# Retention's gated output stored as halves and read in groups, more down-projection tiles kept on chip, and the work around both down projections reordered

## The chip, the cores and the metric

The kernel runs on one core of a Trainium2 chip. The metric is device time of one launch, in microseconds (us); lower is better. The median of three runs of the kernel before is 2861.47 us (2861.45 to 2865.29).

## The reference

One inference step of a two-layer streaming encoder over T = 1056 rows (1024 prompt rows of a new stream and 32 rows of a running one), all in float32, model width D = 1024:

```
layer 0:  x += Retention(RMSNorm(x));  x += ConvFFN(RMSNorm(x))
layer 1:  x += GLA(RMSNorm(x));        x += ConvFFN(RMSNorm(x));  then a final RMSNorm
retention: q, k, v, g = h @ w_in; per head S = gamma^L S + k^T v, o = intra + q S
           out = (silu(g) * groupnorm(o)) @ w_out          (w_out: 2048 x 1024, "w_ro")
gla:       the same form with gates per channel; out = (silu(r) * rmsnorm(o)) @ w_out   (1024 x 1024, "w_go")
conv_ffn:  u = h @ w_up; a causal convolution of width 3; silu(gate) * val @ w_down
```

The outputs are y, the new retention and GLA states and the new convolution caches.

## The kernel before, in words

TensorE multiplies float32 as sums of shorter products: each factor is split into a high half (a cast on ACT) and a low half (a subtraction on DVE), and each product is three matmuls (high x high, high x low, low x high; lines 1311 to 1313 in `Down.run`). A weight tile is 128 x 1024 ("K tile", 512 KB): `load_w` (L97 to 102) loads it into one of three `raw` tiles and splits it into `whi` and `wlo`, out of a ring of ten `w` tiles.

The stages, in us of the profiled execution: projections of the retention to 349; four retention heads of 87 us each to 697; the retention's down projection to about 900; FFN up and down of layer 0 to 1630; GLA to 2045; its down projection to about 2129; FFN of layer 1 to the end. The change touches the heads, both down projections and the two entries to an FFN.

**The heads** (`retention`, L440 and on). Each head goes through nine steps of 128 rows (eight of the prompt, one of the sample). A step computes scores, output and state update on TensorE; DVE and ACT normalise the output (`output`: bn_stats L585, square root L589, `on` L599); a step later `norm` transposes it (`pt`, L604), multiplies it by the gate (`ot`, L609) and stores it to HBM as float32 (`scr_or`, L610). `update` (L630) forms the new state `Sn`. The last head's last gated tile stands in a kept `w` tile named `or`. While the last steps run, `early` (L1250) already loads and splits K tiles 0 and 1 of the down projection, and `order` pins some of those instructions behind others on the same engine. PSUM banks have tags (`sm`, `v`, `out`, two buffers each, and a projection bank).

**The down projections** (class `Down`, L1242 to 1363). The rows go in four chunks of 264 (`CQ`). For each chunk `run` goes through the K tiles (16 of w_ro, 8 of w_go), each with eight output tiles, so 24 matmuls of 264 columns per K tile, and accumulates in eight PSUM banks. In layer 0, `load` fetches a K tile's 132 KB of gated output (`HR<-scr_or`, L1285), splits it (`XH`, L1286 and L1287) and loads and splits its weights. K tiles 5 to 7 of w_ro (0 to 2 of w_go) stay on chip in `XB` after their first use; all others are loaded again for each chunk. In layer 1 the gated output is stored as halves already (`scr_hg`), and a 1056 KB group of four K tiles comes by one load on POOL's queue (L1278). At a chunk's last K tile each output tile is evicted right behind its matmuls (`evict`: residual added on DVE, L1498; square sums on ACT; two tiles at a time stored to `scr_x` by POOL, L1502). The next chunk starts with its first tiles (`hold`: four) in seven banks; the eighth holds the row sum `pn` of the chunk before (L219), from which DVE (`rm`, L225) and ACT (L164, L165) form 1/rms, `R`. Then `done` scales the chunk by the norm's weights and R, eight DVE instructions of 128x264 (L1515), and `x_sums` (L288 to 293) forms and splits the sums and differences for the FFN. Such deferred pieces are emitted two or three per K tile (`later`).

**The entry to an FFN** (`ffn_up`, L1365). Its products use seven instead of eight block products (`seven`), with sums of weights (`weight_sums`: L312 to 323) and of x. `weight_sums(0)` is called when the down projection has been emitted; the last chunk's norm comes behind the fourth product.

A scheduler places the instructions of each engine by emission order and priority; `order` adds constraints. Each engine and each DMA queue (SP's, POOL's) then runs in order.

Of the kernel before, what the change touches and what calls it, by code (L numbers as in the profile page):

```python
# [50 lines left out]
def trunk_kernel(ctx: ExitStack, tc: tile.TileContext, io):  # L51
# [45 lines left out]
    def load_w(src, dst=None, after=None, queue=nc.sync):  # L97
        i = uid()
        raw = raw_tile(f"raw{i}")
        queue.dma_start(raw, src)  # L100
# [111 lines left out]
    def rms_row(ss, c0, n, ps, after=None, join=False):  # L212
# [12 lines left out]
        V.tensor_scalar(m_, ps, 1.0 / D, EPS, op0=ALU.mult, op1=ALU.add)  # L225
        rsqrt(r_, t_, m_)

# [152 lines left out]
    scr_o = [io["scr_or"], io["scr_og"]]  # L380
# [34 lines left out]
    def retention():  # L415
# [29 lines left out]

        def rsm(name):
            return pp.tile([P, 512], F32, tag="sm", name=name, bufs=2)
# [18 lines left out]
        for h in range(RH):  # L466
# [5 lines left out]
            def before(m):  # L472
# [15 lines left out]
                if samp and h + 1 == RH:  # L488
                    kept = w_tile("or").bitcast(F32)
                    sg = kept[:, RDV:RDV + 4 * L].rearrange("p (e t) -> p e t", e=4)  # L490
# [4 lines left out]
                pss = pp.tile([P, 512], F32, tag="sm", name=f"pss{i}", bufs=2)  # L495
# [13 lines left out]
                pk = pp.tile([P, 2, P], F32, tag="sm", name=f"pk{i}", bufs=2)  # L509
# [16 lines left out]
                psv = pp.tile([P, RDV], F32, tag="v", name=f"psv{i}", bufs=2)  # L526
# [29 lines left out]
            def output(ctx):  # L556
# [12 lines left out]
                po = pp.tile([P, RDV], F32, tag="out", name=f"po{i}", bufs=2)  # L569
# [7 lines left out]
                else:  # L577
# [7 lines left out]
                V.bn_stats(bs[:L], po[:L])  # L585
# [7 lines left out]
                V.scalar_tensor_tensor(ab[:L, 3:4], mv[:L, 0:1], -1.0, ab[:L, 2:3],  # L593
                                       op0=ALU.mult, op1=ALU.mult)
                if kept is not None:
                    on = kept[:, :RDV]
# [4 lines left out]
                def norm(sm, i=i, on=on, L=L, t0=t0, h=h, sg=sg, kept=kept):  # L601
# [3 lines left out]
                    if kept is not None:  # L605
                        ot = kept[:, RDV + 4 * L:RDV + 8 * L].rearrange("p (e t) -> p e t", e=4)
                    else:
                        ot = rp.tile([P, 4, P], F32, tag="ot", name=f"ot{i}", bufs=2)
                    V.tensor_tensor(ot[:, :, :L], pt[:, :, :L], sg, op=ALU.mult)  # L609
# [3 lines left out]
                return last_root, ts, last_on  # L613

            def update(ctx, after=None):
# [20 lines left out]
                if m >= 7:  # L636
                    dst = io["o_ret_p"] if m == 7 else io["o_ret_s"]
                    nc.sync.dma_start(dst[h].rearrange("(d p) e -> p d e", p=P), sn)
# [7 lines left out]
            root7, ts7, on7 = output(c7)  # L646
# [7 lines left out]
        norms[0](lambda name: pp.tile([P, 512], F32, tag="v", name=name, bufs=2))  # L654
# [253 lines left out]
    def gla(closers):  # L908
# [147 lines left out]
        def mix(h, c, u):  # L1056
# [109 lines left out]
            def store(lv, room):  # L1166
                for e in range(2):
# [5 lines left out]
                    nc.sync.dma_start(scr_o[1][2 * h + e, :, c0:c0 + n], ot[:, :n])  # L1173
# [68 lines left out]
    class Down:  # L1242
        def __init__(self, nk, wsrc, hsrc, chunks, res, sm, keep, hold):
# [3 lines left out]
            self.banks = self.after = self.groups = None  # L1247

        def early(self, kt, after=None, wafter=None):
# [4 lines left out]
            h = w_tile(f"hs{uid()}")  # L1254
            ins = (S.copy(h[:, :n], hr),
                   V.tensor_tensor(h[:, 512:512 + n], hr, h[:, :n].bitcast(F32), op=ALU.subtract))
            if after is not None:
                for a, b in zip(ins, after):
                    order(a, b)
# [504 lines left out]
```

## Time and profile before

| | us |
|---|---|
| median of 3 runs | 2861.47 |
| profiled execution | 2860.82 |
| its span, first to last instruction | 2859.0 |
| TensorE (PE) busy | 2818.5, 99% |
| VectorE (DVE) busy | 1976.2, 69% |
| ScalarE (ACT) busy | 1333.7, 47% |
| GpSimd (POOL) busy | 297.7, 10% |

The page gives one execution: busy time by engine, the granted clock of TensorE, DMA, groups of instructions by line. Views of the trace answer for a stretch: busy time, what an engine waited for, single instructions in time. Matmuls overlap in the pipeline, so a matmul's own duration (0.28 us for 264 columns) is longer than the pace at which they start.

### The profile page before, as it was taken

What the parts mean: (1) busy time and instruction counts of PE and PEld (TensorE: products, weight loads), DVE (VectorE), ACT (ScalarE), POOL (GpSimd) and SP (SyncE); (2) the same over time, 40 slices, a digit from 0 to 9 for tenths busy, and PEclk for the clock granted to TensorE, in tenths of its full rate; (3) what the DMA queues carried; (4) which work ended last, traced back from release to release, by engine and by line L of the source; (5) the groups of instructions that cost most, each with busy time, mean ns of one, the idle gap of its engine ahead of it and who ended that gap; (6) DMA issues with size and microseconds to landing.
All of it is one profiled execution on the core that took longest, in us unless ns stands there. A gap on an engine that the chain in (4) does not pass through costs nothing.

```text
span 2859.0 us, 51822 instructions
## 1 busy us (share of the span) xinstructions
PE 2818.5 (99%) x20670; PEld 2721.2 (95%) x20670; DVE 1976.2 (69%) x3313; ACT 1333.7 (47%) x2402; POOL 297.7 (10%) x558
## 2 busy tenths in 40 slices
PE   9999999999999999999999999999999999999998
PEld 8999988887999999999999999999989999999998
DVE  7876666666688878787555677775488777876544
ACT  7444444444554444444444555553344444444443
POOL 0000000000020111111000122220131111110000
PEclk9999999999999999999999999999999999999999
DMA  5333444333873222223755411115651222227544
GB/s 221 100 117 105 148 120 131 106 107 113 276 227 120 82 83 75 83 75 114 251 186 174 129 37 41 46 44 199 230 180 60 90 68 90 69 81 250 184 155 145
DMA packets 199890, 365.72 MB, mean 128 GB/s; under 512 B 34976, under 2 KB 133408, under 8 KB 198368
## 3 DMA queue, kind: packets, MB, share of 16 engines
q1 hardware_dynamic: 195232, 344.00, 37.2%
q0 software_dynamic: 3856, 17.83, 1.8%
q8 instruction: 161, 2.64, 0.4%
q14 instruction: 81, 0.66, 0.1%
q10 hardware_dynamic: 560, 0.59, 0.1%
HBM read 279.07 MB, written 83.28 MB: 127 GB/s over the span
## 4 chain that ended last, share of the span: by engine, by line
PE 89%; DVE 6%; DMA 2%; ACT 2%; issue 1%; SPq 0%; POOL 0%; DVEq 0%; ACTq 0%; POOLq 0%
PE pu L357 14%; PE pu L352 13%; PE pu L356 13%; PE pd L1311 8%; PE pd L1312 7%; PE pd L1313 7%; PE psv L245 2%; PE psv L246 2%; PE psv L247 2%; PE pj L770 1%; DMA raw<-w_ro 1%; PE pg L123 1%; PE pg L124 1%; PE pl L1024 1%; PE pg L125 1%; PE pj L123 1%
## 5 line engine op out<-in xcount | busy, mean ns | idle before, releaser
L102 DVE TENSOR_TENSOR wlo<-raw,whi 128x1024 fp32r<-128x1024 f32 x226 | 282.1, 1251 | 247.9 <-ACT whi L102 237.3
L102 ACT CAST whi<-raw 128x1024 fp32r<-128x1024 f32 x226 | 236.0, 1049 | 319.5 <-PE pd L1312 227.5
L1311 PE MATMUL pd<-hh,whi 128*128 128x384 f32 (+1 forms) x880 | 285.0, 324 | 0.0
L1312 PE MATMUL pd<-hl,whi 128*128 128x384 f32 (+1 forms) x880 | 284.3, 323 | 0.1
L1313 PE MATMUL pd<-hh,wlo 128*128 128x384 f32 (+1 forms) x880 | 283.9, 323 | 0.0
L333 ACT COPY HR<-pu 128x264 f32<-128x264 f32 x264 | 98.9, 375 | 313.1 <-PE pu L357 310.6
L357 PE MATMUL pu<-XA,wgl 128*128 128x264 f32 x752 | 213.4, 284 | 0.0
L352 PE MATMUL pu<-XA,wgh 128*128 128x264 f32 x752 | 212.6, 283 | 0.0
L356 PE MATMUL pu<-XA,wgh 128*128 128x264 f32 x752 | 212.4, 283 | 0.0
L1312 PEld LDWEIGHTS pd<-hl,whi 128*128 128x128 f32 x880 | 165.7, 188 | 0.9 <-DVE hl L1287 0.4
L1311 PEld LDWEIGHTS pd<-hh,whi 128*128 128x128 f32 x880 | 165.7, 188 | 0.4
L1394 DVE SCALAR_TENSOR_TENSOR AR<-AR,cw 128x1058 f32<-128x1058 f32 x88 | 115.9, 1317 | 72.3 <-ACT AR L1393 72.3
L1313 PEld LDWEIGHTS pd<-hh,wlo 128*128 128x128 f32 x880 | 165.6, 188 | 0.1
L1311 PE MATMUL pd<-XH,whi 128*128 128x264 f32 x560 | 160.2, 286 | 0.5 <-DMA XH<-scr_hg 0.5
L1313 PE MATMUL pd<-XH,wlo 128*128 128x264 f32 x560 | 158.9, 284 | 0.0
L1312 PE MATMUL pd<-XH,whi 128*128 128x264 f32 x560 | 158.8, 284 | 0.1
L313 DVE TENSOR_TENSOR wtl<-rv,wth 128x1024 fp32r<-128x1024 f32 x58 | 71.0, 1225 | 117.1 <-ACT wth L312 115.4
L1374 DVE TENSOR_TENSOR AR<-HR,pu 128x264 f32<-128x264 f32 (+2 forms) x440 | 144.5, 367 | 4.6 <-PE pu L357 4.6
L352 PEld LDWEIGHTS pu<-XA,wgh 128*128 128x128 f32 x752 | 141.2, 188 | 0.0
L356 PEld LDWEIGHTS pu<-XA,wgh 128*128 128x128 f32 x752 | 141.2, 188 | 0.0
L357 PEld LDWEIGHTS pu<-XA,wgl 128*128 128x128 f32 x752 | 141.0, 188 | 0.0
L352 PE MATMUL pu<-XA,wsh 128*128 128x264 f32 x464 | 132.3, 285 | 4.4 <-ACT wsh L312 3.2
(483 smaller groups left out, 9585.3 us busy)
## 6 DMA issues: line engine op xcount, KB each, us to landing
raw<-w_down SPq DMA_DIRECT2D x120, 512.0 KB, 3.6
raw<-w_ro SPq DMA_DIRECT2D x55, 512.0 KB, 4.5
rg<-w_up SPq DMA_DIRECT2D x44, 512.0 KB, 3.5
rv<-w_up SPq DMA_DIRECT2D x44, 512.0 KB, 3.5
scr_h<-AR SPq DMA_DIRECT2D x44, 512.0 KB, 2.6
HR<-scr_h SPq DMA_DIRECT2D x84, 192.0 KB, 3.6
raw<-w_go SPq DMA_DIRECT2D x23, 512.0 KB, 4.0
scr_x<-AR POOLq DMA_DIRECT2D x32, 264.0 KB, 4.0
```

The costliest lines, as they stand in the source:

```text
L102: ins = S.copy(hi, raw), V.tensor_tensor(lo, raw, hi.bitcast(F32), op=ALU.subtract)
L123: PE.matmul(ps, hi[:, k], rh, start=kt == 0, stop=False)
L313: V.tensor_tensor(l_, src, h.bitcast(F32), op=ALU.subtract)
L333: S.copy(t, b)
L352: mm = PE.matmul(ps, wh[:, k], x[:, 0, kt], start=m in (1, 2, 4, 5) and kt == 0, stop=False, skip_group_check=True)
L356: PE.matmul(ps, wh[:, k], x[:, 1, kt], start=False, stop=False, skip_group_check=True)
L357: mm = PE.matmul(ps, wl[:, k], x[:, 0, kt], start=False, stop=kt == 3, skip_group_check=True)
L1311: PE.matmul(o, w[0][:, k], h[0][:, :n], start=i == 0, stop=False)
L1312: PE.matmul(o, w[0][:, k], h[1][:, :n], start=False, stop=False)
L1313: self.last_mm = PE.matmul(o, w[1][:, k], h[0][:, :n], start=False, stop=i == nk - 1)
L1374: V.tensor_tensor(u[:, d:d + n], t[:, o:o + n], b[:, o:o + n], op=op)
L1394: V.scalar_tensor_tensor(cj, uj[:, 1:T + 3], cw[:, nt, 1:2], cj, op0=ALU.mult, op1=ALU.add)
```

## The change

1. `norm` in the heads gates in place, splits the result (an ACT cast and a DVE subtraction of 128x512 per step, 35 in all, into one buffer `hl`) and stores both halves to `scr_hr`, laid out by chunk and group (44 stores, since a step that crosses a chunk's border is stored in two). The down projection of layer 0 then reads groups of 1056 KB by POOL, as layer 1 does: 16 loads instead of 62 of 132 KB, and no splits. The state stores of the last head go by POOL's queue.
2. More weights stay on chip. In layer 0, K tiles 3 and 8 to 11 stay through chunk 1, 2 and 4 through chunk 2, 5 to 7 throughout, with a new order of K tiles in chunks 1 to 3: w_ro is loaded 46 times instead of 55. In layer 1 all eight tiles of w_go stay: 8 loads instead of 23. Every fourth load of layer 0's chunks 1 to 3 goes into `HR`, free now, as a fourth raw tile (7 loads).
3. Orders and banks at the last head's end: seven PSUM tags in fixed places (`bank`), state updates and weight splits behind the last two steps' `bias`, the gating of step 7 ahead of the last update; chunk 0 starts in two halves of four banks instead of three and five.
4. Orders in the chunks: the eight evictions come behind all eight matmul groups, the next chunk's first two low halves behind the last eviction and later ones behind `rm`, and the next chunk's groups are asked for ahead of time, the stores to `scr_x` behind them on POOL. Layer 1 holds three K tiles instead of four before `pn`.
5. `weight_sums(0)` of the FFN is emitted inside the last chunk, two K tiles before its last in layer 1, before the last in layer 0. In the order of DVE's instructions, layer 0's sums stood ahead of the last evictions before as well, layer 1's did not.
6. The norm's weights g are multiplied on by ACT (eight of 128x264 per chunk, in `pre`, ahead of the row sum), and R by DVE in two instructions of 128x1056.

TensorE's instructions are the same in number. The core of the diff:

```diff
-                    V.tensor_tensor(ot[:, :, :L], pt[:, :, :L], sg, op=ALU.mult)
-                    nc.sync.dma_start(scr_o[0][4 * h:4 * h + 4, :, t0:t0 + L].rearrange("e p t -> p e t"),
-                                      ot[:, :, :L])
+                    gated = V.tensor_tensor(ot[:, :, :L], pt[:, :, :L], sg, op=ALU.mult)
+                    if after is not None:
+                        order(gated, after)
+                    cast = S.copy(hl[:, :, 0, :L], ot[:, :, :L])
+                    V.tensor_tensor(hl[:, :, 1, :L], ot[:, :, :L], hl[:, :, 0, :L].bitcast(F32), op=ALU.subtract)
...
+                        nc.sync.dma_start(io["scr_hr"][c, h, :, :, :, o:o + n], hl[:, :, :, a:a + n].bitcast(F32))
...
-            sn7 = update(c7, ts7)
+            sn7 = update(c7, ts7 if h + 1 < RH else bias7)
...
-                d1s[0].early(1, (root7, ts7), (root7, sn7))
-                d1s[0].after = on7, sn7
-            output(c8)
-            update(c8)
+                d1s[0].early(1, (root7, sn7))
+            _, _, bias8 = output(c8)
+            if h + 1 == RH:
+                d1s[0].after = last_on, bias8
+                norms[0](lambda name: bank("v", name), bias8)
+            update(c8, bias8 if h + 1 == RH else None)
...
+        def group(self, c, q):
+            if (c, q) not in self.groups:
+                h = self.room("hq").rearrange("p (k j t) -> p k j t", k=4, j=2)
+                self.asked = G.dma_start(h, self.gsrc(c, q))
+                self.groups[c, q] = h
+            return self.groups[c, q]
...
+            w = self.kept.get(kt)
+            if w is None:
+                dst = self.room("kw") if kt in self.keep else None
+                if c == 0 and kt in self.homes:
+                    home = self.homes[kt][0]
+                    dst = home[:, :D], home[:, D:2 * D]
...
+                if self.put is not None:
+                    self.count += 1
+                    after = None, self.put if self.count < 3 else self.rm
+                    self.loads += 1
+                    if self.spare is not None and self.loads % 4 == 3:
+                        raw = self.spare[:, :D], self.steps[-5]
+                elif self.spare is not None and kt in range(4, 7):
+                    after = self.gated
+                w = load_w(self.wsrc(kt), dst, after, raw=raw)
+                if dst is not None or self.stay:
+                    self.kept[kt] = w
...
+                    if ask and i == nk - 3:
+                        self.group(c + 1, ask[0])
...
+                    if c == len(self.chunks) - 1 and i == nk - 1 and not self.stay:
+                        nxt_sums()
                     if prev is None or i > J:
                         for nt in range(KT):
                             mm(i, nt)
-                            if i == nk - 1:
-                                evict(c, nt, xr[:, nt], ps[nt][:, :n], ss)
+                        if c == len(self.chunks) - 1 and i == nk - 3 and self.stay:
+                            nxt_sums()
+                        if i == nk - 1:
+                            if ask:
+                                self.group(c + 1, ask[1])
+                            for nt in range(KT):
+                                self.put, self.count = evict(c, nt, xr[:, nt], ps[nt][:, :n], ss), 0
...
+                            if pre is not None:
+                                pre(last)
+                            dg[0] = self.rm = norm_a(c - 1, prev)
...
+            def pre(xr):
+                for kt in range(KT):
+                    S.activation(xr[:, kt], xr[:, kt], AF.Copy, scale=gcol[:, idx, kt:kt + 1])
...
-                        V.scalar_tensor_tensor(a, a, gcol[:, idx, kt:kt + 1], R[:, c0:c0 + n],
-                                               op0=ALU.mult, op1=ALU.mult)
...
+                        V.tensor_tensor(a, a, R[:, c0:c0 + n].unsqueeze(1).to_broadcast([P, 4, n]), op=ALU.mult)
...
+            go([lambda after: (pre(xr), norm(3, ss, after))] + done(3, xr), down.early, d1.last_mm)
...
+    d1s[0].kts = {c: [5, 6, 7, 4, 2, 3, 0, 1] + list(range(8, 16)) for c in range(1, 4)}
+    d1s[1].stay, d1s[1].kts = True, {3: [3, 0, 1, 4, 5, 6, 7, 2]}
+    d1s[0].banks = (0, 1, 2, 3), (4, 5, 6, 7)
```

More of the change, by code (lines that the diff above doesn't have):

```diff
@@ L95, in w_tile, with load_w @@
         return wp.tile([P, D], F32R, tag="w", name=name, bufs=10)
-    def load_w(src, dst=None, after=None, queue=nc.sync):
+    def load_w(src, dst=None, after=None, queue=nc.sync, raw=None):
         i = uid()
-        raw = raw_tile(f"raw{i}")
-        queue.dma_start(raw, src)
+        behind = None
+        if raw is None:
+            raw = raw_tile(f"raw{i}")
+        else:
+            raw, behind = raw
+        load = queue.dma_start(raw, src)
+        if behind is not None:
+            order(load, behind)
         hi, lo = dst or (w_tile(f"whi{i}"), w_tile(f"wlo{i}"))
@@ L1301, in run @@
                     kts = list(keep) + [k for k in kts if k not in keep]
+                kts = self.kts.get(c, kts)
+                for k, (_, end) in self.homes.items():
+                    if c > end:
+                        self.kept.pop(k, None)
                 J = self.hold
@@ L1533, in second_room @@
+            ss, todo, xr = d1.run(droom, evict, norm, None, done, (), sums, pre)
+            later(todo, len(todo))
+            go([lambda after: (pre(xr), norm(3, ss, after))] + done(3, xr), down.early, d1.last_mm)
         def second_room(dp):
```

193 lines of the change are left out of this document (104 added, 89 removed).

## The prediction

> **What bounds the kernel now.** I read the head of the page first, then a table of busy time by stretch around the two places that the change touches (the down projection of the retention, 697 to 930 us, and that of the GLA with the entry to its FFN, 1960 to 2165 us), and then TensorE's own list of waits in both.
>
> ```profile
> span 2859.0 us, 51822 instructions
> PE 2818.5 (99%) x20670; PEld 2721.2 (95%) x20670; DVE 1976.2 (69%) x3313; ACT 1333.7 (47%) x2402; POOL 297.7 (10%) x558
> ```
>
> TensorE is busy for 2818.5 of 2859.0 us. The change takes no matmul away, so only idle and slowly clocked stretches can be won. The columns of the next table are the stretch, its length, busy time and instructions of PE, PEld, DVE, ACT and POOL, the granted clock, the DMA share and GB/s.
>
> ```profile
> 610.00:697.00 87.00, 86.81 (x423) 70.54 (x422) 54.45 (x129) 33.63 (x67) 0.00 (x0) 1.00 0.28 79
> 697.00:721.00 24.00, 21.25 (x156) 18.70 (x155) 14.27 (x28) 12.52 (x19) 0.33 (x2) 1.00 0.80 268
> 721.00:749.00 28.00, 28.00 (x233) 28.00 (x232) 17.05 (x24) 14.77 (x24) 0.00 (x0) 1.00 0.93 300
> 749.00:757.00 8.00, 6.08 (x49) 5.68 (x48) 7.28 (x15) 5.85 (x13) 3.41 (x5) 1.00 0.81 254
> 757.00:800.00 43.00, 43.00 (x355) 42.94 (x354) 30.02 (x49) 20.55 (x33) 4.14 (x7) 1.00 0.79 270
> 800.00:850.00 50.00, 48.77 (x398) 48.28 (x397) 41.61 (x60) 28.77 (x48) 13.05 (x17) 1.00 0.63 202
> 900.00:926.00 26.00, 23.03 (x169) 22.04 (x169) 23.94 (x36) 9.75 (x16) 1.43 (x2) 0.95 0.12 38
> 2070.00:2113.00 43.00, 42.19 (x344) 41.59 (x343) 37.05 (x56) 20.93 (x33) 16.50 (x23) 1.00 0.71 236
> 2113.00:2119.00 6.00, 4.52 (x36) 4.25 (x35) 5.97 (x8) 2.76 (x5) 4.24 (x8) 1.00 0.35 105
> 2131.00:2142.00 11.00, 7.07 (x34) 6.53 (x34) 8.48 (x11) 4.93 (x9) 2.53 (x4) 0.69 0.47 156
> 2152.00:2165.00 13.00, 10.69 (x79) 9.63 (x78) 12.12 (x14) 6.92 (x9) 0.00 (x0) 1.00 0.12 42
> ```
>
> The stretch from 757 to 800 is the undisturbed pace: 43.00 us for 355 matmuls of 264 columns, 0.1211 us each, so 2.91 us for the 24 of a K tile. Against that pace each stretch loses its length less its matmuls times 0.1211: 2.1 us at 749 (8 - 49 x 0.1211), 1.8 at 800 to 850, 5.5 at 900 to 926, 1.3 at 2070 to 2113, 1.6 at 2113 to 2119, 6.9 at 2131 to 2142 and 3.4 at 2152 to 2165. At 697 to 721 other shapes are mixed in, and I take the idle time, 2.75. In sum 25.4 us can be won, 0.9% of the run. Part of it is no wait but clock: at 900 to 926 a granted 0.95 costs 26 x 0.05 = 1.3 us, at 2131 to 2142 a granted 0.69 costs 3.4.
>
> What TensorE waits for, first from 697 to 930, then from 2060 to 2165 (total, times, longest, in us):
>
> ```profile
> PE pd L1311 <- DVE AR L1498: 3.0, 3, 1.5
> PE pu L352 <- DVE AR L1374: 1.3, 2, 1.1
> PE pt L604 <- ACT or L599: 1.1, 1, 1.1
> PE pd L1311 <- DVE Sn L630: 1.0, 1, 1.0
> PE pu L352 <- ACT HR L333: 0.9, 1, 0.9
> PE pu L356 <- DVE XB L289: 0.7, 1, 0.7
> PE pt L604 <- ACT on L599: 0.6, 1, 0.6
> ```
> ```profile
> PE pu L352 <- ACT wsh L312: 3.2, 1, 3.2
> PE pd L1311 <- DVE rm L225: 1.5, 1, 1.5
> PE pu L352 <- ACT HR L333: 0.9, 1, 0.9
> PE pd L1311 <- DMA XH<-scr_hg: 0.5, 1, 0.5
> ```
>
> They are handovers between stages: the last head to the down projection (or, Sn, on), eviction of a chunk's last banks (L1498), the norm chain into the FFN (L1374, L289, L333), and in layer 1 the split of the FFN's weight sums (wsh). None is throughput of DVE or ACT.
>
> **The heads: 0 us.** Each 128-row step gains an ACT cast and a DVE subtraction of 128x512, priced by the same shapes:
>
> ```profile
> 562.38 0.69 DVE L609 TENSOR_TENSOR ot<-pt,sg 128x512 f32<-128x512 f32 x1 [2.67 <-PE pt L604]
> 562.00 0.59 ACT L540 CAST vh<-psv 128x512 fp32r<-128x512 f32 x1 [2.89 <-PE psv L247]
> ```
>
> So 0.59 us more on ACT and 0.69 on DVE per step, against idle stretches of 2.89 and 2.67 us just before these rows: the cover is about 2 us a step, and the head's 87 us keep 0.2 us of idle. If that cover were gone, 35 steps would cost up to 1.28 us each, 45 in all; I take 0, bounded by +2 for the few steps that carry weight splits too. The stores double to 512 KB:
>
> ```profile
> scr_or<-ot SPq DMA_DIRECT2D x32, 256.0 KB, 2.4
> raw<-w_ro SPq DMA_DIRECT2D x55, 512.0 KB, 4.5
> XH<-scr_hg POOLq DMA_DIRECT2D x6, 1056.0 KB, 6.0
> scr_x<-AR POOLq DMA_DIRECT2D x32, 264.0 KB, 4.0
> AR<-xT SPq DMA_DIRECT2D x4, 1056.0 KB, 9.2
> ```
>
> At 2.4 us for 256 KB an estimate for 512 KB is 4.8, and the single buffer is wanted again after 87/9 = 9.7 us, on queues that are 0.28 busy. The fixed PSUM banks leave TensorE's order in the heads as it was.
>
> **Entry to the down projection: -1.0 us (-2.7 to +1.3).** on (0.6) and Sn (1.0) should go: the last two steps' biases now stand ahead of the state updates on DVE, and K tile 0 gets four banks that aren't held by Sn. The wait for or (1.1) stays and may grow: its gating on DVE now comes behind a 0.69 subtraction, and ACT has 0.59 ahead of it. I count -1.6 + 0.6. The last state stores move from SP's to POOL's queue; the first write into the room that they free is the split of K tile 4, some ten us later, against a landing like the 4.0 of POOL's other stores.
>
> **Chunk feed: 0 us.** Per chunk the 16 loads of 132 KB and their splits become four POOL loads of 1056 KB that need no splits, and w_ro falls from 55 loads to 46, w_go from 23 to 8. In chunk 0 it is no relief: 24 us x 268 GB/s + 28 x 300 = 14.8 MB moved from 697 to 749; now 14 x 0.13 = 1.9 MB go and 2.1 to 4.2 come (two groups can be fetched before 697). At 300 GB/s that is 1 to 8 us more of transfers in a stretch that was 0.93 busy. With a K tile per 2.91 us a group feeds 11.6 us, and 6.0 to 9.2 us of landing fit, so I take 0, and keep the price of the miss for the rivals.
>
> **Chunk boundaries: -3.3 us in layer 0 (-3.9 to -1.5), -2.0 in layer 1 (-2.9 to -0.5).** The eight evictions now go to DVE back to back, and the next chunk's first splits are held behind the last of them, where before a split stood between. What is lost at 749 and 800 to 850 is 3.9 us; I leave 0.2 per boundary. In layer 1 (2.9 lost) w_go stays on chip, so no split is left there at all; but the norm's row sum is asked for after three K tiles (8.7 us) instead of four, which may be early for its last sum on POOL. I leave 0.3 per boundary. Next to that, ACT gets eight scalings per chunk; behind them stand weight splits that the order places K tiles ahead of need.
>
> **Exit of layer 0: -0.9 us (-2.5 to +2).** The scaling falls from 8 instructions to 2:
>
> ```profile
> L102 DVE TENSOR_TENSOR wlo<-raw,whi 128x1024 fp32r<-128x1024 f32 x51 | 64.1, 1259 | 18.5 <-ACT whi L102 18.4
> L1515 DVE SCALAR_TENSOR_TENSOR AR<-AR,gcol,R 128x264 f32<-128x264 f32 x32 | 13.7, 486 | 0.0
> L293 DVE TENSOR_TENSOR AR<-AR 128x1056 f32<-128x1056 f32 x8 | 10.0, 1249 | 0.0
> ```
>
> 8/32 of 13.7 is 3.4 us; two of 128x1056 take 2.5. The 0.9 gained comes off the waits for XB (0.7) and HR (0.9). For it, ACT does eight scalings (0.4 each by the same width, 3.3 in all) ahead of the row's square root, and they wait for the stores of x, the last issued here:
>
> ```profile
> 899.81 0.72 POOL L1502 DMA_DIRECT2D scr_x<-AR  x1
> ```
> ```profile
> 905.65 0.42 ACT L164 ACTIVATE rt<-rm 128x264 f32<-128x264 f32 x1 [4.15 <-DVE rm L225]
> ```
>
> ACT was idle for 4.15 us before that root, and 899.81 + 0.72 + 4.0 + the last two scalings ends at 905.4: it just fits. A landing some 2 us later is the +2. The weight sums of this exit move hardly at all in the order, so no more than this is won.
>
> **Exit of layer 1: -5.7 us (-8.5 to -2).** Here the order does change: the FFN's first weight sums, which stood behind the last evictions, now come three K tiles (8.7 us) before the chunk's end, and with all of w_go on chip DVE has no weight split (1.26 us each) in between. That is the order that layer 0's exit already has, so I price it by that: 6.9 + 3.4 = 10.3 us lost now, against 5.5 at 900 to 926, less the 0.9 of the scaling, so 4.6 stays. Of wsh's 3.2 nothing stays; next late is the norm chain.
>
> Beside this row of the granted clock (0.69) stands a rule of the Trainium skill. "TensorE: Matmul & The Clock Gate", What's actually happening, says that the clock halves after an idle window of about 3.4 us. Here it was 0.95 at 900 to 926, where no single wait passed 1.3 us, so this trace shows dips after less. By the rule both exits would lose their dips, the third rival below.
>
> **The sum.** -1.0 - 3.3 - 2.0 - 0.9 - 5.7 = -12.9 us. The profiled execution took 2860.82 us (1.8 around the span): 2847.9. The median of 2861.47 is 0.65 above that: **2848.6 us**, 0.45% faster. A measurement of this kernel tells about 0.2%, 5.7 us, from no change.
>
> **The rivals.**
> 1. Handovers move rather than go (0.20, about 2856). wsh's 3.2 us are won and half of the boundaries (2.6), and the chain of norm, x sums and splits sets the exits as before, dips included: -5.8. For it: DVE is busy for 23.94 of 26 us at layer 0's exit with the early order. Against: layer 0's exit loses half as much as layer 1's. Half of this chance falls under the 0.2%.
> 2. Bursts shut out the weights: slower (0.15, about 2877). A 1056 KB group comes at once where 132 KB came per K tile. With four raw tiles a weight is asked for 4 x 2.91 = 11.6 us ahead. If its 512 KB queue behind a whole burst, 4.5 + 9.2 = 13.7 us, TensorE waits 2.1 us, at 14 of the 16 groups 29 us; less 12.9, +16. It decides from a landing of 11.6; the change is slower by over 0.2% from 12.9. Against: the six bursts of layer 1 land in 6.0 and cost one wait of 0.5 us. For: 0.93 DMA share in chunk 0.
> 3. No dips at the exits (0.08, about 2845): the 1.3 us of layer 0 go too, and about as much of layer 1, -12.9 - 2.6 = -15.5.
> 4. The change doesn't bite (0.05, 2861): the waits at the evictions were not the split's doing, and the weight sums' loads come late too.
>
> **How the numbers follow.** The forecast has 0.52, its own bounds some 2841 to 2855. The range of 8 in 10 takes in rivals 1, 3 and 4 and ends before rival 2: **2840 to 2863**. Faster by over 0.2% (under 2855.7): 0.52 + 0.10 + 0.08 + 0.03 of rival 2's smaller sizes = 0.73; within: 0.10 + 0.05 = 0.15, less 0.01 for tails; slower: 0.13.
>
> **What would show it.** Right: no wait on the evictions over 0.3 us at the four boundaries, wsh gone from TensorE's waits in layer 1 and its exit losing under 6 us, heads still at 86.8 of 87, XH groups landing in 6 to 9 us. Wrong: waits of TensorE on whi with raw from w_ro behind them, on XH groups, or on the new scaling through R at the exits; a wait on the or gating over 2 us; idle time of TensorE inside the heads.

## The result and the profile after

| | before | after |
|---|---|---|
| median, same chip (5 runs each) | 2861.47 us (2859.51 to 2865.88) | 2876.82 us (2873.97 to 2882.95) |
| ratio | | 1.0051, 95% interval 1.0035 to 1.0067 |
| span of the profiled execution | 2859.0 | 2875.0 |

The change makes the kernel 0.51% slower, where 0.45% faster was forecast. The head of the page of the changed kernel:

```profile
span 2875.0 us, 51538 instructions
PE 2821.5 (98%) x20670; PEld 2725.7 (95%) x20670; DVE 1932.4 (67%) x3213; ACT 1333.3 (46%) x2414; POOL 316.5 (11%) x578
```

DVE has 44 us less to do and 100 instructions fewer, TensorE the same 20670 matmuls, and the span is 16.0 us longer. What TensorE waits for in the changed kernel, from 697 to 930 us and then from 2040 to 2165 (total, times, longest):

```profile
PE pd L1367 <- DMA XH<-scr_hr: 12.7, 1, 12.7
PE pd L1367 <- DVE or L628: 2.4, 1, 2.4
PE pu L359 <- DVE AR L1446: 1.4, 1, 1.4
```
```profile
PE pn L225 <- POOL ss L221: 7.3, 3, 3.2
PE pu L359 <- DVE AR L1446: 1.1, 1, 1.1
```

Nearly every wait of the lists of before is gone: the evictions, Sn, on, HR and XB in layer 0, wsh, rm, HR and the group of layer 1; of the norm chain into the FFN, AR at line 1446 (1374 before) stays. Five waits, of three kinds, are new or longer: one for a group of the gated output, one for the gating `or`, and three for `ss` at line 221, the sum on POOL that joins two halves of a chunk's squares ahead of the row sum `pn`. A sixth, of 0.3 us, is for a half sum (`ss`, L154). The table by stretch shows where the pace is lost (stretch, length, PE, PEld, DVE, ACT, POOL, granted clock, DMA share, GB/s):

```profile
610.00:697.00 87.00, 86.18 (x419) 69.94 (x418) 59.06 (x136) 39.71 (x78) 1.58 (x3) 1.00 0.51 143
706.00:710.00 4.00, 1.61 (x9) 1.41 (x9) 2.06 (x4) 1.95 (x3) 0.74 (x1) 0.82 0.79 264
710.00:715.00 5.00, 5.00 (x24) 5.00 (x24) 1.89 (x2) 2.94 (x3) 0.00 (x0) 0.50 0.97 304
721.00:749.00 28.00, 28.00 (x233) 28.00 (x233) 9.80 (x8) 8.41 (x8) 1.29 (x3) 1.00 1.05 382
837.00:850.00 13.00, 0.52 (x5) 0.31 (x3) 3.78 (x4) 1.90 (x2) 5.49 (x9) 0.68 0.84 301
850.00:855.00 5.00, 4.79 (x22) 4.82 (x23) 0.00 (x0) 0.00 (x0) 0.00 (x0) 0.50 0.18 71
```

The heads and the steady part of chunk 0 stay at their pace. From 837 to 850 TensorE stands still, and from 850 to 855 it runs at half its clock: 22 matmuls in 5 us where 41 fit. The same, smaller, at 706 to 715.

To place every microsecond I took the start of the same matmul (by its number among the 264-column ones of a down projection, or of the heads) in the trace of each kernel. The table gives each stage's length less that of before, in us, for the changed kernel and for the experiments below:

| stage | after | e1 | e2 | e6 | e7 | e8 | e9 | e11 |
|---|---|---|---|---|---|---|---|---|
| up to the heads (code unchanged) | 1.0 | 3.1 | 0.2 | 0.4 | -0.4 | 2.1 | -1.9 | -1.6 |
| heads | 0.8 | 0.2 | 0.2 | 0.3 | 0.5 | 0.8 | 0.4 | 0.4 |
| entry, to K tile 2 of chunk 0 | 1.4 | 1.4 | 0.6 | -2.7 | -2.7 | 1.2 | 1.3 | -2.7 |
| rest of chunk 0 and its boundary | -1.3 | -2.5 | -1.7 | 0.5 | 0.6 | -2.4 | -2.5 | 1.4 |
| chunk 1 | -0.5 | -0.5 | -0.5 | -0.5 | -0.5 | -0.5 | -0.5 | -0.5 |
| chunk 2 | **13.6** | -1.6 | 14.0 | 13.9 | -1.6 | 13.3 | 12.5 | -1.6 |
| chunk 3 | -0.3 | -0.3 | -0.3 | -0.3 | -0.3 | -0.3 | -0.3 | -0.3 |
| exit of layer 0 | -1.4 | -1.6 | -1.7 | -1.6 | -1.4 | -1.5 | -1.6 | -0.7 |
| FFN and GLA (code unchanged) | 3.2 | 3.2 | 0.0 | 3.3 | 0.0 | 0.0 | 3.2 | 0.1 |
| layer 1, chunk 1 | **2.6** | 4.0 | 0.0 | 2.1 | 0.0 | 2.2 | 0.0 | 0.0 |
| layer 1, chunk 2 | **3.4** | 2.6 | 0.0 | 3.9 | -0.3 | 3.3 | 2.1 | -1.0 |
| layer 1, chunk 3 | 0.4 | -0.2 | -0.7 | 0.7 | -0.5 | 12.6 | 1.1 | -1.0 |
| exit of layer 1 | -6.9 | -6.9 | -5.2 | -6.8 | -5.5 | -7.3 | -7.0 | -5.5 |

Two rows are of code that the change leaves alone, and they differ between the profiled executions, one of each kernel (-1.9 to +3.1, and 0 or 3.2): differences of some 3 us between the spans of single executions say little. The traces show most of the 3.2: at the start of the GLA, with DVE, ACT and POOL in the same order, TensorE waits 1.3 us for `A` (L1048) instead of 0.3, and the granted clock is 0.89 over 30 us (from 1640) instead of 0.94 (from 1627 in the kernel before), 1.5 us by that. e1, e6 and e9 have both; e2, e8 and e11 have the short wait; e7 has the long one at a granted 1.00 and comes out even. The median of the changed kernel's five runs has an interval of 0.16% to either side, 4.6 us, so differences of 5 us between two kernels' medians are read together with the stages.

**The 13.6 us of chunk 2.** The group that TensorE waits for at 837 is asked for by POOL. POOL's instructions in the changed kernel (start, length, line, operation; in brackets the idle time before it and what ended it):

```profile
815.63 0.57 POOL L1302 DMA_DIRECT2D XH<-scr_hr  x1 [3.97 <-PE pd L1369]
829.38 11.44 POOL L1453 COPY AR<-cc 128x2 f32<-128x2 f32 x1 [13.19 <-DVE AR L300]
840.76 0.56 POOL L1302 DMA_DIRECT2D XH<-scr_hr  x1
```

Between two group loads stands a copy of two columns per partition, an edge of the convolution's buffer in the FFN's first block (`AR<-cc`). It waits for the x sums of a chunk before (L300), whose tile it reuses, and then takes 11.44 us. The group behind it is asked for at 840.76 and is needed at 837. Before, the copy stood there too, with no load behind it:

```profile
828.30 3.74 POOL L1381 COPY AR<-cc 128x2 f32<-128x2 f32 x1 [20.06 <-DVE AR L293]
```

The copy's own size is not the reason for its length; all copies of this line in the changed kernel (shortest, median and longest in ns):

```profile
L1453 POOL COPY AR<-cc x88: 184/184/11437, 829.4 to 2579.2; 128x2 f32<-128x2 f32 x88
```

While it runs, DVE executes ten instructions with two SBUF inputs each, back to back; these are the first and the last of them:

```profile
829.17 1.22 DVE L108 TENSOR_TENSOR wlo<-raw,whi 128x1024 fp32r<-128x1024 f32 x1
...
838.42 2.36 DVE L108 TENSOR_TENSOR wlo<-raw,whi 128x1024 fp32r<-128x1024 f32 x2
```

DVE's run ends at 840.78 and the copy at 840.82. The Trainium skill, "SBUF — State Buffer", SBUF: two separate sides, states that VectorE and GpSimd share a port pair as an exclusive lock, which a VectorE instruction with two SBUF inputs takes against a GpSimd one that reads SBUF. The trace agrees with the lock: the copy ends 0.04 us behind a VectorE instruction. The same section of the Trainium skill says that whichever starts first has the pair for the whole instruction. By one instruction the copy would wait about 1.2 us, and here it waited for a run of ten. Other copies of this line did get through behind a single one, with the next already begun; this is one for layer 1's FFN, and the DVE instruction that had started before it ended:

```profile
2120.77 1.21 POOL L1453 COPY AR<-cc 128x2 f32<-128x2 f32 x1 [5.28 <-issue]
2121.85 1.25 DVE L296 TENSOR_TENSOR XA<-AR,XA 128x1056 fp32r<-128x1056 f32 x1
```

What decides between one instruction and the whole run is open.

**The three waits in layer 1.** POOL's instructions at the first boundary, in the changed kernel:

```profile
2071.82 0.60 POOL L1302 DMA_DIRECT2D XH<-scr_hg  x1
2072.45 1.59 POOL L1576 DMA_DIRECT2D scr_x<-AR  x2
...
2074.77 0.72 POOL L1576 DMA_DIRECT2D scr_x<-AR  x1
2075.51 0.77 POOL L154 TENSOR_TENSOR ss<-ss,sq 128x264 f32<-128x264 f32 x1
2079.75 0.73 POOL L1576 DMA_DIRECT2D scr_x<-AR  x1 [3.47 <-issue]
2080.51 0.75 POOL L221 TENSOR_TENSOR ss<-ss,ss 128x264 f32<-128x264 f32 x1
```

The join L221 is ready to run at 2076.3, but the fourth store of the residual stands ahead of it, and that store does not start. The four stores' landings in this stretch:

```profile
DMA to landing us min/median/max: 2.6/6.5/7.0
```

The first store, at 2072.45, is the one of 7.0 us: it has landed at 2079.4, and the fourth starts at 2079.75. The same holds at all eight chunk ends of the changed kernel and at the four of layer 0 in the kernel before: the fourth starts 0.31 to 0.33 us after the first has landed. In layer 1 before, the fourth came 0.7 to 4.5 us after that landing, so it did not wait for it there. The first store of a chunk in layer 1 landed after 2.6 to 4.9 us then and lands after 6.6 to 7.9 us now, at the three boundaries where a group load stands ahead of it; and with three K tiles held instead of four TensorE asks for `pn` 2.9 us earlier.

**The entry.** The instructions of ACT around the wait for `or`, and then those of DVE, in the changed kernel:

```profile
705.33 1.28 ACT L213 ACT_TABLE_LOAD   x1
706.62 1.04 ACT L108 CAST XA<-raw 128x1024 fp32r<-128x1024 f32 x1
```
```profile
707.70 1.23 DVE L108 TENSOR_TENSOR XA<-raw,XA 128x1024 fp32r<-128x1024 f32 x1 [1.36 <-ACT XA L108]
708.84 0.28 DVE L628 TENSOR_TENSOR or<-pt,or 128x128 f32<-128x128 f32 x1
```

The gating of 0.28 us stands behind a weight split (K tile 2) that waits for its ACT half, which in turn stands behind a table load.

### The profile page after: what moved, and what is told of

Its sections match the earlier page's. It is cut to its first block, busy times and chain, and to the rows that moved or that the text cites. A ratio compares the mean times of both kernels' runs of the same rounds, so it can differ in the third digit from the quotient of the medians.

```text
span 2875.0 us, 51538 instructions
## 1 busy us (share of the span) xinstructions
PE 2821.5 (98%) x20670; PEld 2725.7 (95%) x20670; DVE 1932.4 (67%) x3213; ACT 1333.3 (46%) x2414; POOL 316.5 (11%) x578
## 4 chain that ended last, share of the span: by engine, by line
PE 87%; DVE 6%; issue 3%; ACT 2%; DMA 1%; POOL 1%; SPq 0%; DVEq 0%; POOLq 0%; ACTq 0%
PE pu L364 13%; PE pu L359 13%; PE pu L363 13%; PE pd L1367 8%; PE pd L1368 7%; PE pd L1369 7%; PE psv L252 2%; PE psv L253 2%; PE psv L254 2%; PE pj L800 1%; PE pl L1054 1%; PE pv L252 1%; PE pv L253 1%; PE pj L129 1%; PE pg L129 1%
## 5 line engine op out<-in xcount | busy, mean ns | idle before, releaser
L108 DVE TENSOR_TENSOR wlo<-raw,whi 128x1024 fp32r<-128x1024 f32 x188 | 233.6, 1246 | 231.0 <-ACT whi L108 220.3
L108 ACT CAST whi<-raw 128x1024 fp32r<-128x1024 f32 x188 | 196.4, 1048 | 285.4 <-PE pd L1368 219.7
L1367 PE MATMUL pd<-XH,whi 128*128 128x264 f32 x432 | 125.3, 290 | 12.7 <-DMA XH<-scr_hr 12.7
L359 PE MATMUL pu<-XA,wth 128*128 128x264 f32 x464 | 131.8, 284 | 1.3 <-ACT wth L319 1.3
L364 PE MATMUL pu<-XA,wsl 128*128 128x264 f32 x464 | 132.1, 285 | 0.1
```

The source lines that it names most:

```text
L108: ins = S.copy(hi, raw), V.tensor_tensor(lo, raw, hi.bitcast(F32), op=ALU.subtract)
L359: mm = PE.matmul(ps, wh[:, k], x[:, 0, kt], start=m in (1, 2, 4, 5) and kt == 0, stop=False, skip_group_check=True)
L364: mm = PE.matmul(ps, wl[:, k], x[:, 0, kt], start=False, stop=kt == 3, skip_group_check=True)
L1367: PE.matmul(o, w[0][:, k], h[0][:, :n], start=i == 0, stop=False)
```

## The experiments

The theory: three handovers cost the time, each of them a matter of what stands ahead of a short instruction in an engine's order: the edge copies on POOL (Q), the fourth store on POOL (layer 1's boundaries), the split on DVE (entry). The rival for chunk 2 (B): the burst of 1056 KB itself is late, because its slot comes free late or its transfer is slow.

**e1.** The edge memsets and copies of the FFN's first two blocks come behind the last group load:

```diff
-                G.memset(u[:, :, 0:2], 0.0)
+                edge = [G.memset(u[:, :, 0:2], 0.0)]
                 for j in range(2):
-                    G.tensor_copy(u[:, j, TP + 2:TP + 4], cc[:, j * NF + f])
+                    edge.append(G.tensor_copy(u[:, j, TP + 2:TP + 4], cc[:, j * NF + f]))
+                if f < 2:
+                    for e in edge:
+                        order(e, d1s[l].asked)
```

> The changed kernel, with the FFN's first edge copies and memsets on POOL (L1451, L1453, for the first two blocks) ordered behind the last group load of the down projection. Theory Q (POOL's in-order queue: the group of chunk 2's last four K tiles stood behind one copy of 128x2 that ran 11.4 us): the one wait of 12.7 us of TensorE for XH goes and with it the half clock behind it (about 2.5 us), so some 15 us less, 2862 us. Rival B (bursts of 1056 KB and the weights share the DMA engines and something lands late whatever the order): the wait stays or moves to another K tile, 2874 to 2877.

Measured: 2860.89 us (11 runs), against 2862.23 for the kernel before (24 runs), ratio 0.9993 (0.9984 to 1.0002): 15.9 us below the changed kernel. The load in question in e1:

```profile
826.53 0.56 POOL L1302 DMA_DIRECT2D XH<-scr_hr  x1 [10.11 <-PE pd L1369]
```

The load that came at 840.76 comes at 826.53, when TensorE has freed its slot; the wait and the half clock behind it are gone, and chunk 2 is 1.6 us shorter than before the change. Q holds, B falls: the same burst, asked for in time, is in time.

**e5.** In the first two blocks of layer 0 the copy is a memset of the same columns, which reads no SBUF; this leaves out the convolution's cache there.

```diff
+                    if l == 0 and f < 2:
+                        G.memset(u[:, j, TP + 2:TP + 4], 0.0)
+                    else:
                         G.tensor_copy(u[:, j, TP + 2:TP + 4], cc[:, j * NF + f])
```

> The changed kernel with the same order on POOL, but the edge copies of the first two FFN blocks of layer 0 replaced by memsets of the same 128x2 (the convolution's cache is left out for these blocks). Theory L (the copy reads SBUF while VectorE runs ten instructions with two SBUF inputs back to back, and waits for their end): the memset takes 0.1 to 0.2 us once its wait for L300 is over at 829.4, the group is issued near 829.6 and lands at 836 to 839, TensorE waits 0 to 2 us instead of 12.7, about 2863 us. Rival (the copy's 11.4 us were a wait for VectorE's sums that no record shows): the memset waits as long, TensorE still loses 12 us, 2875.

Measured: one run, 2857.95 us. POOL in e5:

```profile
828.39 0.09 POOL L1454 MEMSET AR<- 128x2 f32 x1 [12.99 <-DVE AR L300]
829.10 0.56 POOL L1302 DMA_DIRECT2D XH<-scr_hr  x1 [0.62 <-issue]
```

The memset waits for the same x sums, until 828.39, but takes 0.09 us in the midst of DVE's run, and the load follows at 829.10, early enough. So of the two things that the copy does to the queue, the wait for L300 alone would have cost nothing; the 11.44 us decide, and they belong to reading SBUF while DVE reads two inputs.

**e2.** Layer 1 holds four K tiles ahead of `pn` again, instead of three: `range(0, 3), 3)` becomes `range(0, 3), 4)`.

> The changed kernel with four K tiles held in layer 1 before the row sum, as before, instead of three. Theory J (the row sum's join on POOL stands behind the fourth store to scr_x, which starts only when the first has landed, 2 to 3 us after the sum is due at three K tiles): the three waits of pn for ss (7.3 us) go, and the half clock near 2108 (1.7 us), so 9 us less, 2868 us. Rival: the squares or the group loads are late themselves, then a wait of 1 to 2 us per chunk stays and the gain is 3 us at most, 2874.

Measured: 2866.50 us (11 runs), ratio 1.0012 (1.0003 to 1.0021), 10.3 below the changed kernel. The waits of e2 in this stretch:

```profile
PE pn L225 <- POOL ss L221: 1.8, 2, 1.0
PE pn L225 <- DVE ss L154: 1.3, 1, 1.3
```

7.3 us became 3.1; with the clock behind them the three chunks take 0.7 less than before the change, not 6.4 more. The exit gains 1.7 less with four tiles held. Of the 11.2 us between the two profiled executions these 5.4 are the edit's, and 4.0 lie in the two stages of unchanged code; so the 10.3 of the medians, near the 9 us that were expected, is more than the stages give to the edit.

**e9.** The join L221 goes to DVE in layer 1, with three tiles held.

```diff
-            G.tensor_tensor(ss[0][:, :n], ss[0][:, :n], ss[1][:, :n], op=ALU.add)
+            (V if join > 1 else G).tensor_tensor(ss[0][:, :n], ss[0][:, :n], ss[1][:, :n], op=ALU.add)
```

> The changed kernel, three K tiles held, with the join of the square sums in layer 1 (L221) on VectorE instead of POOL. Theory J (the join is late only because it stands on POOL behind the fourth store to scr_x, which starts when the first has landed): the three waits for ss go whole, 7.3 us and the half clock of 1.7, so 9 to 10 us less, 2867 us, as with four tiles held or a little better. Rival (the squares themselves are late): 1 to 3 us less, 2874.

Measured: 2867.60 us (11 runs), against 2862.95 (17 runs), ratio 1.0016 (1.0008 to 1.0025), 9.2 below the changed kernel, of which the boundaries of layer 1 hold 3.2 in the table (6.4 less 3.2). The join no longer stands behind the fourth store, and no wait for it is left; but among e9's waits there is a new one:

```profile
PE pd L1367 <- DVE AR L1571: 3.2, 1, 3.2
```

That is an eviction: a later handover of the same boundary is late next. What held it can be followed in the trace of e9, to ACT's instructions after that row sum (`rm` is done on DVE at 2097.73):

```profile
2098.18 2.55 ACT L1586 ACTIVATE AR<-AR,gcol 128x264 f32<-128x264 f32 x6 [5.87 <-DMA scr_x<-AR]
2100.64 0.41 ACT L170 ACTIVATE rt<-rm 128x264 f32<-128x264 f32 x1
```

Six of the eight scalings by g stand ahead of the square root, and they begin when the first store of x has landed. So R is late, and DVE's scalings by R and x sums, which follow it nearly without a pause from 2103.78 to 2115.80, run ahead of the evictions. No run moves the scalings with three tiles held, so what they cost there isn't measured.

**e6.** At the entry the split of K tile 2 comes behind the gating of `or`; one DVE instruction changes its place.

```diff
+                elif self.spare is not None and kt == 2:
+                    after = after[0], self.gated[1]
                 elif self.spare is not None and kt in range(4, 7):
```

> The changed kernel with one instruction of VectorE moved: the gating of the last head's last tile (or, L628) stands ahead of the low half of K tile 2 instead of behind it. Theory O (TensorE's wait of 2.4 us near 708 is the order on VectorE: or stands behind a split that waits for ScalarE's table load and cast): the wait goes, and if it was what halved the clock for 6.8 us behind it, 3.4 us more: 2.4 to 5.8 us less, 2871 to 2874 us. Rival: K tile 2 is the late thing there and TensorE then waits for its low half: at most 0.5 us, 2876.

Measured: 2871.62 us (7 runs), ratio 1.0029 (1.0018 to 1.0039), 5.2 below the changed kernel, with intervals that just touch. In the stages 4.1 us are gained at the entry and 1.8 given back in the rest of chunk 0. A stretch of e6 at the entry:

```profile
706.00:715.00 9.00, 8.97 (x74) 8.76 (x73) 3.79 (x4) 2.70 (x4) 0.55 (x1) 1.00 1.01 307
```

74 matmuls in the 9 us where the changed kernel had 33, and no half clock. From 728 to 749, where the changed kernel was busy throughout, TensorE now waits for low halves of weights, and the split of one of them waits for its load:

```profile
PE pd L1371 <- DVE wlo L108: 1.2, 2, 0.8
PE pd L1371 <- DVE XA L108: 0.5, 1, 0.5
736.63 1.05 ACT L108 CAST whi<-raw 128x1024 fp32r<-128x1024 f32 x1 [6.32 <-DMA raw<-w_ro]
```

So the late entry had hidden 1.7 us of late weights in chunk 0.

**e4.** In layer 1 the FFN's first weight sums are emitted behind the whole down projection, as before the change.

```diff
-            ss, todo, xr = d1.run(droom, evict, norm, None, done, (), sums, pre)
+            ss, todo, xr = d1.run(droom, evict, norm, None, done, (), sums if l == 0 else lambda: None, pre)
             later(todo, len(todo))
+            if l == 1:
+                sums()
```

> The changed kernel with layer 1's first FFN weight sums emitted behind the down projection again, as before the change. If the early sums made the exit's gain (7 us between the last K tile of w_go and the FFN, by the two traces): +6 to +7 us, 2883. Rival: the gain came from the scaling in two instructions and from w_go staying on chip, so DVE is free anyway: +0 to +1.5 us, 2877 to 2878.

Measured: 2872.04 us (8 runs), ratio 1.0035 (1.0023 to 1.0047); the exit of layer 1 is still 6.6 us shorter than before, so the loss that was expected did not come. DVE at that exit in the kernel before, with the last eviction and the sums:

```profile
2130.86 0.41 DVE L1498 TENSOR_TENSOR AR<-AR,pd 128x264 f32<-128x264 f32 x1
2135.59 1.21 DVE L313 TENSOR_TENSOR wsl<-rg,wsh 128x1024 fp32r<-128x1024 f32 x1
```

and in e4, with the sums and the first evictions:

```profile
2143.32 1.22 DVE L320 TENSOR_TENSOR wsl<-rg,wsh 128x1024 fp32r<-128x1024 f32 x1
2144.58 1.23 DVE L320 TENSOR_TENSOR wtl<-rv,wth 128x1024 fp32r<-128x1024 f32 x1
2145.72 1.78 DVE L1571 TENSOR_TENSOR AR<-AR,pd 128x264 f32<-128x264 f32 x5
```

The sums run ahead of the evictions although they are emitted behind them: the scheduler moves them up by itself. That it can do so because no weight split is left is an inference from this run and the kernel before, which differ in more than that.

**e8.** w_go is loaded again for each chunk, with the early sums kept (`stay` False, no order of its own for chunk 3; the two conditions on `stay` that place the sums go by the number of K tiles).

> The changed kernel with w_go loaded and split again for each chunk of layer 1 (tiles 0 to 2 kept, as before the change), K tiles in the order before; the FFN's first sums are emitted where the change puts them. The run with the sums emitted late had the same order on VectorE and the same exit, so: theory K (what frees the exit is that the last chunk has no splits): the exit loses its 6 to 7 us again, 2883 us. Rival (the early place of the sums holds them ahead even beside splits): +0 to +2 us, 2877 to 2879.

Measured: 2882.19 us (5 runs), ratio 1.0071 (1.0058 to 1.0083). The size is about what was expected, its place is not: the exit stays 7.3 us shorter, and chunk 3 loses 12.6. ACT in e8, with two casts of the sums ahead of that of the chunk's own weight, which had landed at 2143.8:

```profile
2147.00 1.04 ACT L319 CAST wsh<-rg 128x1024 fp32r<-128x1024 f32 x1 [2.56 <-DVE rg L326]
2147.95 1.04 ACT L319 CAST wth<-rv 128x1024 fp32r<-128x1024 f32 x1
2148.90 1.04 ACT L108 CAST whi<-raw 128x1024 fp32r<-128x1024 f32 x1
```

and the wait that comes of it, behind which the granted clock is 0.52 from 2150 to 2158:

```profile
PE pd L1367 <- ACT whi L108: 6.8, 2, 6.5
```

Early sums with reloaded weights push the chunk's own splits out. The exit gains whenever the sums run early; with the tiles kept, the chunk doesn't pay for it.

**e7** puts e1, e2 and e6 together. **e11** is e7 with the join on DVE, **e10** is e1 and e6 with the join on DVE and three tiles held.

> The changed kernel with the three mends together: FFN's edge copies behind the last group load, four K tiles held in layer 1, or's gating ahead of K tile 2's low half. If the three losses are separate, they add: 15.9 and 10.3 by the runs of the first two, 2.4 to 5.8 for the third, so 2845 to 2848 us, some 15 us below the kernel before. Rival (a mended stall only lets the next one show): 2852 to 2858.

> The kernel with the three mends (2851.2 us), and the join of the square sums in layer 1 on VectorE instead of POOL. There TensorE still waited 0.8 and 0.9 us for the join with four tiles held. Theory J: these go, 1.7 us less, 2849 to 2850 us. Rival (VectorE's own order delays the join or something behind it): no change or slower, 2851 to 2853.

> The changed kernel with FFN's edge copies behind the last group load, or's gating first and, with three K tiles held, the join on VectorE. By the accounts of the single runs layer 1's down projection and exit come to 3.8 us below the kernel before here, against 6.3 with four tiles held: 2853 to 2854 us. If holding three tiles is the better choice once the join is in time, as the change has it: 2849 or less.

| | median (5 runs) | before, same call | ratio (95%) |
|---|---|---|---|
| e7 | 2851.17 | 2862.95 (17 runs) | 0.9961 (0.9947 to 0.9974) |
| e11 | 2848.80 | 2865.32 (9 runs) | 0.9946 (0.9934 to 0.9959) |
| e10 | 2854.46 | 2865.32 (9 runs) | 0.9959 (0.9946 to 0.9971) |

With three edits of order the change is 0.39% faster than the kernel before, and 0.54% with the join on DVE: e11 is the fastest kernel of this study. Between e7 and e11 the intervals overlap; by the table of stages the join brings 0.7 and 0.5 us in layer 1's chunks 2 and 3. e10 shows no gain from holding three tiles even with the join on DVE; a wait of 3.2 us for an eviction, as in e9, is in its trace too.

**e12** is e7 with g multiplied on DVE in eight instructions per chunk, as before the change, and no scalings on ACT.

> The kernel with the three mends (2851.2 us), with the scaling by the norm's weights back on VectorE: eight instructions of 128x264 per chunk instead of ScalarE's eight and two of 128x1056. By the prediction's step the exit of layer 0 (1.4 us shorter than before the change in the traces) gives back 0.9 us, and that of layer 1 as much: 2852.5 to 2853.5 us. Rival (the exits' gain is not the scaling's): 2851 to 2851.5.

Measured: 2852.89 us (5 runs), ratio 0.9955 (0.9942 to 0.9969). The interval overlaps e7's, so by the whole time nothing is settled. In the stages, the exits gain 1.0 and 4.2 us over before where e7's gain 1.4 and 5.5: the scaling on ACT may be worth 1.7 us at the two exits, one execution against one.

**e13** was to be e7 with each eviction behind its own tile's matmuls and the splits not held, for the boundaries alone. As it was edited, the request for the next chunk's group also came ahead of the last K tile's matmuls in the program; they read that group instead of their own, so its output is not the reference's.

> The kernel with the three mends (2851.2 us), with the evictions issued behind each output tile's matmuls again and the next chunk's splits no longer held behind them or the row sum. By the prediction's step the boundaries of layer 0 give back 3.3 us: 2854.5 us. Rival (the boundaries were freed by there being fewer splits, groups without splits and kept tiles): 0 to 1 us, 2851 to 2852.

Measured: 2898.11 us (4 runs), ratio 1.0114 (1.0100 to 1.0128). Its first two waits are the edit's own:

```profile
PE pd L1369 <- DMA XH<-scr_hr: 18.8, 3, 7.2
PE pd L1369 <- DMA XH<-scr_hg: 17.1, 3, 5.8
```

All six boundaries wait for a load that they had no need of. It tells nothing of the evictions' order, which was not tried by itself.

## Why the prediction was wrong

It gave 2848.6 us in 2840 to 2863 and got 2876.82. The step that failed is **the chunk feed at 0 us**, by "6.0 to 9.2 us of landing fit". The landing did fit: the groups asked for from 690 to 900 us landed in 5.1 to 8.8 us, but for two that were asked for one right behind the other at 840.76 and 841.76 (9.3 and 10.9). Among the DMA issues of the changed kernel (count, KB each, median us to landing) stand the 16 groups of layer 0:

```profile
XH<-scr_hr POOLq DMA_DIRECT2D x16, 1056.0 KB, 6.7
```

But the step looked at the transfer alone, and not at what stands ahead of its issue on POOL's queue: a copy of the FFN that waits and is then locked out for 11.44 us. Chunk 2 lost 13.6 us where -1.6 was to be had (e1), and e1 took 15.9 us off the median. The row of 3.74 us for that copy stood in the trace of before.

Between the forecast's -12.9 and the +16.0 us by which the profiled span grew lie 28.9 us. The group of chunk 2 makes 15.2 of them, the boundaries of layer 1 make 8.4, the entry 2.4 and the unchanged code 4.2; the other terms together come to -1.3. So two more steps failed, each a handover whose place in an engine's order was priced too low. The terms in turn:

- **Heads, 0:** +0.8 us, and 0.2 to 0.8 in the other kernels. Right, within its +2.
- **Entry, -1.0:** +1.4, and outside its bounds of -2.7 to +1.3. "The wait for or stays and may grow" named the place, but priced it by the 0.69 and 0.59 us of the new split. What stood ahead of it was the split of a weight, with a table load ahead of that on ACT: 2.4 us, and a half clock behind it. With that one instruction moved the entry gains the 2.7 of the lower bound (e6), 1.8 of it given back in chunk 0, where weights are late.
- **Boundaries of layer 0, -3.3:** -0.5, -1.6 (e1) and -0.3 for chunks 1 to 3, which is -2.4, and chunk 0's boundary is within a stage that mixes with the entry. No wait on an eviction is left there. The size fits; that it comes from holding the splits back was argued, and no run shows it.
- **Boundaries of layer 1, -2.0:** +6.4. "May be early for its last sum on POOL" was the right risk with the wrong size, 0.3 us per boundary instead of 1.8 to 3.2 and, behind the longest, a half clock: the join stands behind a store that waits for another store's landing (e2, e9). The eight scalings on ACT, which the step put at nothing, delay the next handover once the join is in time (e9).
- **Exit of layer 0, -0.9:** -1.4, near in size. How much of it is the scaling isn't known, since the dip of the clock, 1.3 us, went as well (below).
- **Exit of layer 1, -5.7:** -6.9. Near in size, but the early emission isn't what brings it: the scheduler puts the sums there anyway (e4), and with the tiles kept, the chunk doesn't pay for it (e8).
- **Rivals.** The measured time is that of rival 2, 2877, by another way: no wait on whi stands among TensorE's waits in the down projection of layer 0, and at a DMA share of 1.05 and 382 GB/s TensorE was busy for 28.00 of 28 us. Not 14 groups were late but one, so that the figure agrees is luck. Its mechanism shows only in small: once the entry is in time, chunk 0's weights are late by 1.7 us (e6). Rival 1 held in kind, since handovers took the place of handovers, but at other places than it named. Rival 3 held in its mechanism: both exits lost their dips. These are the two exits in the changed kernel, with a granted clock of 1.00 (0.95 and 0.69 before):

```profile
915.00:950.00 35.00, 32.14 (x252) 31.02 (x252) 31.88 (x44) 19.67 (x32) 3.57 (x6) 1.00 0.12 41
2150.00:2170.00 20.00, 18.61 (x147) 17.92 (x147) 18.86 (x31) 11.70 (x27) 5.63 (x7) 1.00 0.32 107
```

That is 1.3 us of layer 0's exit and about as much of layer 1's that the forecast had kept. Rival 4 falls: every place that the change touches moved.

With the three late orders mended (e7) the changed parts come to -11.7 us in the stages, and the medians differ by 11.8, near the -12.9 that the prediction summed up. In part that is luck: one of the three edits takes back a piece of the change (four tiles held again), and the entry gains more, the boundaries less than was forecast.

Open: what brings on the longer wait and the lower clock at the start of the GLA, and whether the change alters how often; what decides how long a locked-out copy waits; the order of the evictions; the value of g on ACT.

## What to carry to other kernels

Where a load moves to another engine's queue, go through what that engine has ahead of it, instruction by instruction, with the wait of each and not only its length: an in-order queue passes on the wait of a 0.2 us copy to a transfer that TensorE needs. A short instruction whose trace shows one duration many times its median is a warning even while nothing stands behind it. And a handover that was tuned with a slack of one K tile (the fourth tile held, a gating ahead of a split) shall have its slack counted again before that tile is given up.

## What the runs showed of the hardware

- A POOL copy that reads SBUF waited through ten DVE instructions with two SBUF inputs that followed each other without a pause: 11.44 us instead of 0.18. Other copies of the same line got through behind one such instruction, in 1.06 to 1.21 us, with the next already begun. A memset in the place of the first took 0.09 us (e5).
- At the ends of the changed kernel's chunks no more than three of the 264 KB stores from POOL's queue were in flight: the fourth started 0.31 to 0.33 us after the first had landed, and instructions behind it on POOL waited with it.
- The clock fell to 0.50 for the stretch of 710 to 715 after TensorE had been busy for 1.61 of the 4 us before, a wait of 2.4 us. By the Trainium skill, "TensorE: Matmul & The Clock Gate", What's actually happening, an idle window of about 3.4 us is what halves it; here less was enough, and with the wait gone the clock stayed at 1.00 (e6).
- The DMA queues moved 382 GB/s for 28 us in chunk 0; the 300 of before, which the prediction took as the pace, were not their limit.
